# Encoder layer on one core: the last two gate chunks as block products, the retention heads started together, three task steps per unit

## The chip, the cores and the metric

The kernel runs on one core of a Trainium2 chip. The metric is device time in microseconds of one execution. The kernel before takes 1811.38 us (median of three runs, 1810.1 to 1811.63).

## What is computed

One encoder layer over 256 tokens of width 2048, all in float32:

```
h      = rmsnorm(x)
proj   = h @ w_in         -> q,k,v of the neighbourhood attention; q,k,v,gate of the retention;
                             q of the attention into mem; three branch gates of 2048 columns each
o_na   = neighbourhood_attention(...)             8 heads of 128
o_ret  = group_norm(retention both ways) * silu(gate)   8 heads, q/k of 128, v of 256
o_mem  = attention into rmsnorm(mem) @ w_mem_kv   4 heads of 256
merged = sigmoid(g_na) * (o_na @ w_br_na) + sigmoid(g_ret) * (o_ret @ w_br_ret)
         + sigmoid(g_mem) * (o_mem @ w_br_mem)
x      = x + merged @ w_out
x      = x + square(relu(rmsnorm(x) @ w_ff1)) @ w_ff2
```

The change touches the gates g_ret, the retention heads and the order of work around the three branch products.

## The kernel before

**Products and units.** Each float32 operand is split into a high and a low part (`split`, L92: ScalarE copies the high part, VectorE subtracts), and a product is three matmuls (`mm3`, L101: high by high, high by low, low by high). Weights come in 512 KB pieces of 256 rows by 512 columns. One piece for both halves of the tokens is a plain unit: 12 matmuls of 512 columns (`chunk`, L240; `do_mm`, L293). A chunk is 512 output columns; over 2048 rows it has 8 units.

**Block products.** `seven` (L656) computes two chunks at once by seven products of half-size blocks instead of eight, each over 4 pieces: 28 products of 6 matmuls each. For this VectorE adds and subtracts blocks of the activations once (`sums`, L781) and of the weights for every pair. Weight sums are formed partly by accumulating transfers into two rings of two buffers (`b1`, `b2`): a plain load from SP's queue, then one from POOL's queue that adds (`ring_load`, `ring_add`, L670 to L676). The last of them is issued with the split of product m6 (`pre`, L730) and is read by the split of product m7. The order is m1 x4, then per piece m3, m5, m7 of the piece before, m6, m2, m4, and m7 of the last piece at the end. While a set runs, six of the eight PSUM banks belong to it (`open_banks`).

**The list of units.** All units stand in one list, and the loop at the end of the function walks it: for unit i it issues the load of unit i + 4, the split of unit i + 2, runs hooks put at i (`at`, L881), the matmuls of unit i and then `run_tasks(i)`. The order is: attention chunks and the chunks on mem; 16 plain retention units; five sets of block products for the gates of the first two branches and half of the third (140 products), with the other 80 retention units spread among them; two plain gate chunks (16 units, `gate_plain`, L842) for the rest of the third branch's gates; the first branch product (na, 16 units), the second (mem, 16), the third (ret, 32); w_out; the feed-forward, where ff2's plain units are spread among the block products of ff1 in the same way. The gates and the retention's q, v and g go out to DRAM (`spill`) and come back when used (`fetch`); the first two branches' inputs too (`back`, L149), by a hook eight units ahead of the branch. Loads with the split operands' type go through POOL's queue, the others through SP's.

**Tasks.** Work that isn't matmuls of the list is written as generators. Each step names what it wants next ("ps" or "pt", the two kinds of PSUM bank, or nothing) and how many units it must wait; `run_tasks` (L216) gives at most two steps after each unit, and at most one for each kind of bank. A retention group (`ret_group`, L500) fetches its four buffers, waits four units, makes decay factors, takes two steps of transposes, then spawns its two heads and the next group. A head (`ret_head`, L517) has four steps: start, scores, output with group norm (in which VectorE waits for POOL's power step, L167 and L168), transposes. Head h is first read by unit h of the third branch. The first group starts three units behind the block products. The buffers of 4 KB a partition ("quad") are 30.

What the code issues in this order has that order of priority; the framework places an instruction earlier on its queue where its inputs and a buffer are free.

Of the kernel before, what the change touches and what calls it, by code (L numbers as in the profile page):

```python
# [12 lines left out]
F32 = mybir.dt.float32  # L13
F32R = mybir.dt.float32r
AF = mybir.ActivationFunctionType
# [6 lines left out]
NT = S // P  # L22
KT = D // P
# [34 lines left out]
def encoder_layer(ctx: ExitStack, tc: tile.TileContext, a, out):  # L58
    nc = tc.nc
# [32 lines left out]
    def split(hi, lo, src, scale=None):  # L92

        if scale is None:
            nc.scalar.activation(hi, src, AF.Copy)  # L95
            nc.vector.tensor_tensor(lo, src, f(hi), op=ALU.subtract)  # L96
        else:
            nc.scalar.activation(hi, src, AF.Copy, scale=scale)  # L98
            nc.vector.scalar_tensor_tensor(lo, src, scale, f(hi), op0=ALU.mult, op1=ALU.subtract)
# [13 lines left out]
    def quad(name, dt=F32R):  # L113

        return qp.tile([P, 4, S], dt, name=name, tag="quad")
# [4 lines left out]
    def spill(t, name):  # L120

        d = dram.tile([P, 4 * S], F32, name=f"d_{name}")
        nc.sync.dma_start(d, f(t).rearrange("p a s -> p (a s)"))
        return d

    def fetch(d, name, dt=F32):
        t = quad(name, dt)
        (nc.sync if dt == F32 else nc.gpsimd).dma_start(t.rearrange("p a s -> p (a s)"), d)
        return t

    def by_tok(t):

        return t.rearrange("p a s -> p (a s)").rearrange("p (t c) -> p t c", t=NT)

    class Lhs:
# [17 lines left out]
        def at(self, k, n=None, tok=slice(None)):  # L153

            ks = k % 4 if n is None else slice(k % 4, k % 4 + n)
            return [t[:, ks, tok] for t in self.quads(k // 4)]
# [19 lines left out]
    hT = Lhs("hT")  # L176
    r_x = const.tile([P, 8], F32, name="r_x")
# [33 lines left out]
    def spawn(gen, after=()):  # L211
        t = Task(gen, after)
        tasks.append(t)
        return t

    def run_tasks(now, n=2):  # L216

        given = set()
        for t in list(tasks):
            if n == 0:  # L220
                break
            if t.ready(now) and t.want not in given:
                if t.want is not None:
                    given.add(t.want)
                t.step(now)
                n -= 1
                if t.done:
                    tasks.remove(t)

    units = []  # L230
# [9 lines left out]
    def chunk(w, x, nkt, done, to=None, halves=False):  # L240

        nu = nkt // UK
        state = {"halves": halves}
        for u in range(nu):
            (units if to is None else to).append((w, u, x, u * UK, u == 0, u == nu - 1, done, state))
# [66 lines left out]
    def transposes(src, blocks):  # L312
        pt = ps_t.tile([P, 4, P], F32, name="pt")
        for j, b in enumerate(blocks):
            nc.tensor.transpose(pt[:, j, :], src[:, b * P:(b + 1) * P], ident)  # L315
        return pt

    def new_T(name):
        return [quad(f"{name}_{x}") for x in ("hi", "lo")]
# [147 lines left out]
    def decay_factors(g):  # L467

        lg, Fd, V = na_env["lg"], na_env["Fd"], nc.vector
        e1, e2 = cst["dist_f"], cst["dist_b"]  # L470
        Fq = quad("Fd", F32).rearrange("p a s -> p (a s)")
        for h in (2 * g, 2 * g + 1):
            t = t2f("junk")[:, :3 * P]
            Fd[h] = Fq[:, (h % 2) * 3 * P:(h % 2 + 1) * 3 * P]
            V.tensor_scalar_mul(t, e1, lg[:, h:h + 1])
            V.scalar_tensor_tensor(t, e2, lg[:, RET_H + h:RET_H + h + 1], t, op0=ALU.mult, op1=ALU.add)
            nc.scalar.activation(t, t, AF.Exp)
            V.tensor_scalar_mul(Fd[h], t, RET_QK ** -0.5)
# [16 lines left out]
            nc.vector.tensor_tensor(qv[:, :, 0, :], qv[:, :, 0, :], bv[:, :, 0, :], op=ALU.subtract)  # L495
            nc.vector.tensor_tensor(qv[:, :, 1, :], qv[:, :, 1, :], bv[:, :, 1, :], op=ALU.add)

    ret_dram = {}

    def ret_group(g):  # L500

        q2 = by_tok(fetch(ret_dram["q", g], "ret_q"))
        v = [by_tok(fetch(d, f"ret_v_{x}", F32R)) for d, x in zip(ret_dram["v", g], ("hi", "lo"))]
        gs = by_tok(fetch(ret_dram["g", g], "ret_gs"))
        yield None, 4
        decay_factors(g)
        T = new_T("ret_qkT")
        for t in range(NT):
            yield "pt", 1
            pt = transposes(q2[:, t, :], range(4))  # L510
            split(T[0][:, :, t * P:(t + 1) * P], T[1][:, :, t * P:(t + 1) * P], pt)
        for j in range(2):
            spawn(ret_head(2 * g + j, j, T, v, gs, env["oT_ret"]))
        if g + 1 < 4:
            spawn(ret_group(g + 1))

    def ret_head(h, j, qkT, v, gs, oT):  # L517
        Fd = na_env["Fd"]
# [39 lines left out]
    def w_chunk(name, c):  # L558
        return a[name][c]
# [27 lines left out]
    def win(c):  # L587
        return w_chunk("w_in", c)
# [233 lines left out]

    gate_dram = {}

    def put_gate(key, sg):
        yield None, 2
        gate_dram[key] = spill(sg, "sg")

    def gate_pair(key, c, ci, to):
        def finish(e):  # L830
            sgs = [quad("sg", F32) for _ in range(2)]
            for n, sign, ch, t in RESULTS:
                nc.scalar.activation(by_tok(sgs[ch])[:, t, :], e[n], AF.Sigmoid, scale=sign)
                if n == "c12":
                    yield None, 2
            for i in range(2):
                yield None, 2
                gate_dram[key, c + i] = spill(sgs[i], f"sg_{key}{c + i}")

        seven(win(ci), win(ci + 1), x_left, False, r_x, finish, to)  # L840

    def gate_plain(key, c, ci):  # L842
        def done_gate(acc):
            sg = quad("sg", F32)
            for t in range(NT):
                nc.scalar.activation(by_tok(sg)[:, t, :], acc[t], AF.Sigmoid, scale=r_x[:, t:t + 1])
            spawn(put_gate((key, c), sg))

        chunk(win(ci), hT, KT, done_gate)

    def ret_chunks(g, to):
        def put(key, ts, x=""):
# [36 lines left out]
    ret = ret[16:]  # L889
    sv = []  # L890
    for key, c, ci in (("w_br_na", 0, 8), ("w_br_na", 2, 10), ("w_br_mem", 0, 12), ("w_br_mem", 2, 14),
                       ("w_br_ret", 0, 28)):
        gate_pair(key, c, ci, sv)
    n = len(ret)
    for i, x in enumerate(sv):
# [6 lines left out]
        bank.clear()  # L902

    at(len(units) + 1, end_of_seven)
    at(len(units) + 3, lambda: spawn(ret_group(0)))
    for i in range(2):
        gate_plain("w_br_ret", 2 + i, 30 + i)


    def branch(wname, oT_key, nkt, first, last):  # L910
# [153 lines left out]
    for p in range(1, NPAIR):  # L1064
        sv = []
        ff1_pair(p, sv)
        for i, x in enumerate(sv):
            units.append(x)
            if p == 1:
                n = (i + 1) * (16 - LAG) // len(sv) - i * (16 - LAG) // len(sv)  # L1070
            elif i < EARLY:
                n = (i + 1) * LAG // EARLY - i * LAG // EARLY
            else:
                j, m = i - EARLY, len(sv) - EARLY
                r = 16 - LAG - (5 if p == NPAIR - 1 else 0)
                n = (j + 1) * r // m - j * r // m
# [12 lines left out]
    for i in range(n_units):  # L1089
        issue(i + LOADS)  # L1090
        do_split(i + SPLITS)
        for j in range(i, min(i + LEAD + 1, n_units)):
            if isinstance(units[j], Product):
                for lead, fn in units[j].acts:
                    if lead == j - i:
                        fn()
        if i == 20:
            spawn(stats_task(a["mem"], r_m))
        if i == 28:
            spawn(mem_task())  # L1100
        if i == 100:
            spawn(decay_task())
        if i == u_out - 4:
            for c in range(4):
                env["x1", c] = quad_f("x1")
                nc.gpsimd.dma_start(env["x1", c],
                                    a["x"][:, c * CW:(c + 1) * CW].rearrange("(t p) d -> p t d", p=P))
        for fn in hooks.get(i, []):
            fn()
        do_mm(i)  # L1110
        units_done.append(i)
        run_tasks(i)
    i = n_units
    while tasks:
        run_tasks(i)
        i += 1
# [102 lines left out]
```

## Time and profile before

| what | value |
|---|---|
| runs | 1810.1, 1811.38, 1811.63 us |
| the profiled execution | 1808.42 us |
| its span, first to last instruction | 1806.7 us |
| mean granted TensorE clock | 0.998 |
| TensorE, VectorE, ScalarE, POOL busy | 1778.9, 1411.2, 1043.7, 148.5 us |
| moved by DMA | 442.62 MB, 245 GB/s over the span |

TensorE is busy for nearly the whole span, so the table alone does not say where time could come from: for that one reads the idle stretches of TensorE, and how near the other engines are to their limit in each stage. Busy time is the union of an engine's instructions, which overlap at their ends: a matmul of 512 columns lasts some 0.39 us by its own row, and the next one starts sooner.

### The profile page before, as it was taken

The page shows a single profiled execution, that of the slowest core. Times are in us where ns is not written, and L with a number is a line of the kernel's source. Part 1 is how long each engine was busy: PE and PEld are TensorE (multiplying, and loading weights), DVE is VectorE, ACT ScalarE, POOL GpSimd, SP SyncE. Part 2 cuts the span into 40 slices and gives each one's busy share as a digit, 9 for nine tenths or more (in the row PEclk, how much of TensorE's full clock was granted, in tenths as well). Part 3 has the DMA queues.
Part 4 walks back from the last instruction along what each step waited for, and adds up shares of the span by engine and source line. Part 5 has one row for each costly group of instructions (what it writes and reads, how often), then busy time and mean ns, then how long its engine had stood idle before and what let it go on. Part 6 is the DMA issues. An engine that isn't in the chain of part 4 may idle for free.

```text
span 1806.7 us, 22753 instructions
## 1 busy us (share of the span) xinstructions
PE 1778.9 (98%) x8130; PEld 1467.8 (81%) x8130; DVE 1411.2 (78%) x1793; ACT 1043.7 (58%) x1305; POOL 148.5 (8%) x176
## 2 busy tenths in 40 slices
PE   8999999999999999999999999999999999999999
PEld 6888888787888887888788888777888888888877
DVE  6777766988788888868875556887898888888874
ACT  7665554556565665654434455855565656666552
POOL 0101000010001000101010000010111110110100
PEclk9999999999999999999999999999999999999999
DMA  9756555899998999987676555788889888888854
GB/s 328 270 202 229 187 175 198 271 292 293 279 301 239 312 289 279 297 315 284 230 254 211 185 184 180 223 243 222 244 256 267 232 266 246 252 237 281 221 186 140
DMA packets 148866, 442.62 MB, mean 245 GB/s; under 512 B 14096, under 2 KB 14608, under 8 KB 148752
## 3 DMA queue, kind: packets, MB, share of 16 engines
q1 hardware_dynamic: 123952, 377.54, 59.1%
q0 software_dynamic: 24512, 62.92, 18.1%
q8 instruction: 64, 1.05, 0.2%
q10 hardware_dynamic: 288, 0.70, 0.1%
q14 instruction: 50, 0.41, 0.1%
HBM read 420.13 MB, written 20.97 MB: 244 GB/s over the span
## 4 chain that ended last, share of the span: by engine, by line
PE 84%; DVE 8%; DMA 4%; ACT 2%; issue 2%; POOL 0%; SPq 0%; DVEq 0%; ACTq 0%; POOLq 0%
PE acc L103 22%; PE acc L104 22%; PE acc L102 22%; PE ps L104 3%; PE ps L103 3%; PE ps L102 3%; DVE w_lo L96 3%; DMA b<-in_w_ff 3%; PE pt L104 2%; PE pt L102 2%; PE pt L103 2%; ACT w_hi L95 1%; DMA raw<-in_w_ff 1%; PE pt L315 1%; DVE b L680 0%
## 5 line engine op out<-in xcount | busy, mean ns | idle before, releaser
L96 DVE TENSOR_TENSOR w_lo<-raw,w_hi 128x1024 fp32r<-128x1024 f32 (+1 forms) x545 | 660.4, 1221 | 202.5 <-ACT w_hi L95 196.7
L95 ACT ACTIVATE w_hi<-raw 128x1024 fp32r<-128x1024 f32 (+1 forms) x545 | 573.6, 1056 | 373.9 <-PE acc L104 287.6
L95 ACT ACTIVATE w_hi<-b 128x1024 fp32r<-128x1024 f32 x240 | 252.4, 1059 | 261.7 <-PE acc L104 142.7
L96 DVE TENSOR_TENSOR w_lo<-b,w_hi 128x1024 fp32r<-128x1024 f32 x240 | 291.8, 1223 | 114.5 <-ACT w_hi L95 111.9
L102 PE MATMUL acc<-w_hi,hT_hi 128*128 128x512 f32 x744 | 291.8, 394 | 7.6 <-ACT hT_hi L98 5.0
L103 PE MATMUL acc<-w_lo,hT_hi 128*128 128x512 f32 x744 | 291.2, 392 | 4.1 <-DVE w_lo L96 4.1
L104 PE MATMUL acc<-w_hi,hT_lo 128*128 128x512 f32 x744 | 290.5, 391 | 0.0
L103 PE MATMUL acc<-w_lo,fT_hi 128*128 128x512 f32 x512 | 200.7, 392 | 2.3 <-DVE w_lo L96 2.2
L102 PE MATMUL acc<-w_hi,fT_hi 128*128 128x512 f32 x512 | 201.1, 393 | 1.7 <-DVE x L1041 1.3
L104 PE MATMUL acc<-w_hi,fT_lo 128*128 128x512 f32 x512 | 200.1, 391 | 0.0
L102 PEld LDWEIGHTS acc<-w_hi,hT_hi 128*128 128x128 f32 x744 | 140.2, 189 | 37.3 <-ACT hT_hi L98 5.0
L103 PEld LDWEIGHTS acc<-w_lo,hT_hi 128*128 128x128 f32 x744 | 140.3, 189 | 34.0 <-DVE w_lo L96 6.0
L104 PEld LDWEIGHTS acc<-w_hi,hT_lo 128*128 128x128 f32 x744 | 140.2, 188 | 29.3
L103 PEld LDWEIGHTS acc<-w_lo,fT_hi 128*128 128x128 f32 x512 | 96.6, 189 | 24.7 <-DVE w_lo L96 4.9
L102 PEld LDWEIGHTS acc<-w_hi,fT_hi 128*128 128x128 f32 x512 | 96.5, 189 | 22.9 <-DVE x L1041 1.3
L104 PEld LDWEIGHTS acc<-w_hi,fT_lo 128*128 128x128 f32 x512 | 96.6, 189 | 20.0
L664 POOL DMA_DIRECT2D b<-in_w_ff x56 | 67.7, 1255 | 540.9 <-DMA b<-in_w_ff 162.3
L102 PE MATMUL pt<-w_hi,f_S_hi 128*128 128x512 f32 x192 | 75.0, 390 | 1.6 <-ACT w_hi L95 1.6
L103 PE MATMUL pt<-w_lo,f_S_hi 128*128 128x512 f32 x192 | 75.1, 391 | 0.8 <-DVE w_lo L96 0.8
L104 PE MATMUL pt<-w_hi,f_S_lo 128*128 128x512 f32 x192 | 75.0, 390 | 0.0
L664 POOL DMA_DIRECT2D b<-in_w_in x40 | 34.7, 896 | 429.9 <-DMA b<-in_w_in 321.0
L680 DVE TENSOR_TENSOR b<-b,raw 128x1024 f32<-128x1024 f32 x48 | 58.7, 1223 | 2.2 <-DMA raw<-in_w_in 1.2
(295 smaller groups left out, 2939.6 us busy)
## 6 DMA issues: line engine op xcount, KB each, us to landing
raw<-in_w_in SPq DMA_DIRECT2D x215, 512.0 KB, 5.4
raw<-in_w_ff SPq DMA_DIRECT2D x200, 512.0 KB, 5.9
b<-in_w_ff SPq DMA_DIRECT2D x56, 512.0 KB, 5.6
b<-in_w_ff POOLq DMA_DIRECT2D x56, 512.0 KB, 8.5
b<-in_w_in SPq DMA_DIRECT2D x40, 512.0 KB, 5.5
b<-in_w_in POOLq DMA_DIRECT2D x40, 512.0 KB, 7.6
raw<-in_w_mem_kv SPq DMA_DIRECT2D x32, 512.0 KB, 3.2
raw<-in_w_br_ret SPq DMA_DIRECT2D x32, 512.0 KB, 3.7
```

Source lines behind the costliest of these rows:

```text
L95: nc.scalar.activation(hi, src, AF.Copy)
L96: nc.vector.tensor_tensor(lo, src, f(hi), op=ALU.subtract)
L102: nc.tensor.matmul(o, lhsT=lh, rhs=rh, start=start, stop=False)
L103: nc.tensor.matmul(o, lhsT=lh, rhs=rl, start=False, stop=False)
L104: nc.tensor.matmul(o, lhsT=ll, rhs=rh, start=False, stop=stop)
L315: nc.tensor.transpose(pt[:, j, :], src[:, b * P:(b + 1) * P], ident)
L664: eng.dma_start(t.rearrange("p (b c) -> p b c", b=2) if len(src.shape) == 3 else t, src, **kw)
L680: V.tensor_tensor(raw, raw, add, op=ALU.add)
```

## The change

The third branch's last two gate chunks are computed by a sixth set of block products, so that there are 168 products with the 80 retention units among them and no plain gate chunk. The unit behind the last product is then the first branch's first. `ret_group(0)` starts one unit behind the block products instead of three; each group spawns the next in its first step instead of its last, and waits three units instead of four before its decay factors. `ret_built` is an empty list to which nothing is added, so `ret_built[-1:]` names no task to wait for. `run_tasks` gives three steps per unit instead of two, in the whole kernel. The limit of one step for each kind of bank stays.

```
-    def run_tasks(now, n=2):
+    def run_tasks(now, n=3):
...
-    ret_dram = {}
+    ret_dram, ret_built = {}, []
...
         gs = by_tok(fetch(ret_dram["g", g], "ret_gs"))
-        yield None, 4
+        if g + 1 < 4:
+            spawn(ret_group(g + 1), ret_built[-1:])
+        yield None, 3
         decay_factors(g)
...
             spawn(ret_head(2 * g + j, j, T, v, gs, env["oT_ret"]))
-        if g + 1 < 4:
-            spawn(ret_group(g + 1))
...
     for key, c, ci in (("w_br_na", 0, 8), ("w_br_na", 2, 10), ("w_br_mem", 0, 12), ("w_br_mem", 2, 14),
-                       ("w_br_ret", 0, 28)):
+                       ("w_br_ret", 0, 28), ("w_br_ret", 2, 30)):
         gate_pair(key, c, ci, sv)
...
-    at(len(units) + 3, lambda: spawn(ret_group(0)))
-    for i in range(2):
-        gate_plain("w_br_ret", 2 + i, 30 + i)
+    at(len(units) + 1, lambda: spawn(ret_group(0)))
```

The functions `put_gate` and `gate_plain`, now unused, are removed.

## Rows read from the trace of the kernel before

**Rows 1.** The page, busy time, share of the span and instructions of TensorE.
```profile
PE 1778.9 (98%) x8130; PEld 1467.8 (81%) x8130; DVE 1411.2 (78%) x1793; ACT 1043.7 (58%) x1305; POOL 148.5 (8%) x176
```

**Rows 2.** Waits of TensorE, whole span: releaser, us in total, times, longest.
```profile
PE acc L103 <- DVE w_lo L96: 7.0, 7, 1.7
...
PE pt L552 <- DVE ret_qkT_lo L96: 3.6, 3, 1.4
...
PE acc L102 <- DVE junk L493: 1.4, 2, 0.7
```

**Rows 3.** Busy time by stretch; last columns granted clock, DMA share, GB/s.
```profile
335.00:766.40 431.40, 425.84 (x1873) 350.66 (x1872) 368.90 (x370) 261.12 (x273) 38.03 (x47) 1.00 0.92 287
766.40:926.00 159.60, 156.03 (x782) 130.75 (x780) 123.05 (x226) 75.98 (x95) 13.68 (x26) 1.00 0.74 270
1150.00:1240.00 90.00, 86.11 (x373) 68.92 (x372) 73.26 (x79) 54.76 (x67) 10.86 (x9) 0.97 0.90 254
1516.00:1608.00 92.00, 92.00 (x416) 76.20 (x415) 81.50 (x81) 57.41 (x62) 12.07 (x10) 1.00 0.87 250
```

**Rows 4.** TensorE in order of time: start, duration, line, operation.
```profile
762.29 0.39 PE L102 MATMUL pt<-w_hi,f_S_hi 128*128 128x512 f32 x1
...
766.14 0.39 PE L104 MATMUL acc<-w_hi,hT_lo 128*128 128x512 f32 x1
766.37 0.39 PE L102 MATMUL acc<-w_hi,hT_hi 128*128 128x512 f32 x1
...
815.36 0.40 PE L102 MATMUL acc<-w_hi,oT_na_hi 128*128 128x512 f32 x1
...
925.97 0.48 PE L102 MATMUL acc<-w_hi,oT_ret_hi 128*128 128x512 f32 x1
```

**Rows 5.** VectorE: splits in order of time; its wait for POOL; merges, 764 to 960.
```profile
903.54 4.63 DVE L96 TENSOR_TENSOR w_lo<-raw,w_hi 128x1024 fp32r<-128x1024 f32 x4
...
DVE rs_t L169 <- POOL rs_y L168: 8.6, 8, 1.1
...
L929 DVE TENSOR_TENSOR merged<-merged,junk 128x512 f32<-128x512 f32 x10 | 6.7, 686 | 0.0
```

**Rows 6.** DMA queues, 335 to 766 us: packets, MB, share of 16 engines.
```profile
q1 hardware_dynamic: 27180, 98.96, 62.1%
q0 software_dynamic: 6785, 24.72, 29.8%
```

**Rows 7.** POOL's accumulations (L664): landing 335 to 770, 1150 to 1240; one issue.
```profile
DMA to landing us min/median/max: 5.3/7.6/10.5
...
DMA to landing us min/median/max: 6.4/9.0/12.3
...
746.25 0.86 POOL L664 DMA_DIRECT2D b<-in_w_in  x1 [12.78 <-DVE b L680]
```

**Rows 8.** A set's end in the feed-forward: ScalarE, TensorE, then two stretches.
```profile
1230.71 1.06 ACT L95 ACTIVATE w_hi<-b 128x1024 fp32r<-128x1024 f32 x1 [6.14 <-DMA b<-in_w_ff]
...
1231.82 0.49 PE L102 MATMUL pt<-w_hi,f_S_hi 128*128 128x512 f32 x1 [1.59 <-ACT w_hi L95]
1233.07 0.50 PE L103 MATMUL pt<-w_lo,f_S_hi 128*128 128x512 f32 x1 [0.76 <-DVE w_lo L96]
...
1234.00:1236.00 2.00, 1.49 (x4) 0.61 (x2) 2.00 (x5) 1.75 (x3) 1.20 (x1) 0.50 0.81 261
...
1238.00:1240.00 2.00, 2.00 (x6) 1.52 (x6) 2.00 (x4) 1.28 (x2) 0.00 (x0) 0.50 1.06 250
```

**Rows 9.** The first branch's input: one issue on POOL; landing, median us.
```profile
748.37 0.90 POOL L128 DMA_DIRECT2D oT_na_lo<-d_oT_na_lo  x1
...
oT_na_lo<-d_oT_na_lo POOLq DMA_DIRECT2D x2, 512.0 KB, 15.1
```

**Rows 10.** POOL's first power step, 764 to 960 us: count, ns min/median/max.
```profile
L167 POOL TENSOR_SCALAR rs_u<-mv x8: 191/191/1069, 813.3 to 923.8; 128x2 f32<-128x2 f32 x8
```

More of the change, by code (lines that the diff above doesn't have):

```diff
@@ L823, in encoder_layer @@
     gate_dram = {}
-    def put_gate(key, sg):
-        yield None, 2
-        gate_dram[key] = spill(sg, "sg")
     def gate_pair(key, c, ci, to):
@@ L840, in gate_pair @@
         seven(win(ci), win(ci + 1), x_left, False, r_x, finish, to)
[L842 to L849, printed above, removed]
     def ret_chunks(g, to):
```

## The prediction

> **What bounds the kernel now.** I read the page's busy shares first, then who waits for whom on TensorE, then busy time by stage, and only then single instructions. TensorE is busy for 98% of the span [rows 1], and all that it waits for is some 25 us: in the stages that the change touches there are three waits of the last retention step for VectorE (3.6 us), two for an accumulator that VectorE has not emptied (1.4 us) and some late low halves of weights [rows 2]. The granted clock is 1.00 in these stages [rows 3]. So a matmul saved is time saved, as long as VectorE and the DMA keep up, and their margins decide the rest: in the stage of block products (335 to 766 us, with a few plain units ahead of them) VectorE is busy for 368.9 of 431.4 us and the DMA for 0.92; in the stage with the retention heads (766 to 926 us) VectorE has 123.05 us of work beside 156.03 us of TensorE's [rows 3]. I call the first unit after the block products L; in the kernel before it begins at 766.37 us, the first branch product at 815.36 us and the third at 925.97 us [rows 4].
>
> **1. Two plain gate chunks become one set of seven block products.** Eighteen matmuls of 512 columns start between 762.29 and 766.14 us, so one costs 3.85 / 17 = 0.2265 us, in a block product and in a plain unit alike [rows 4]. Plain: 2 chunks x 8 units x 12 matmuls = 192, or 43.5 us. Block products: 28 x 6 = 168, or 38.1 us. All lie on TensorE's path: **-5.4 us**.
>
> What comes with them: VectorE gets 28 splits and 8 adds of the same shape at 1.16 us and seven combinations at 0.67 us [rows 5], 46 us beside 38.1 us of matmuls, so its share of the stage goes from 0.855 to (368.9 + 46) / 469.5 = 0.88. The DMA took 2.71 us a MB for plain loads and 5.20 for the queue of accumulating ones (62.1% of 431.4 us for 98.96 MB, 29.8% for 24.72 MB [rows 6]); 16 loads and 8 accumulations of 0.524 MB are 22.7 + 21.8 = 44.5 us in 38.1, and the share goes from 0.92 to 0.94. Both stay covered on average.
>
> The Trainium skill (Perfetto Trace Analysis, section Roofline) names some 435 GB/s as the most that a core's 16 DMA engines move; by that the 287 GB/s of this stage would leave a third free and the late transfers of rival 3 would have no cause. The rows differ: the same engines are at 0.92 already, since an accumulated byte holds them nearly twice as long, so I keep the rival at its full chance.
>
> **2. The same 80 retention units among 168 products instead of 140.** Before, a plain unit follows the one before it after one or two products; now always after two or more (80 / 168 is under a half). The two waits for an emptied accumulator, 0.7 us each [rows 2], have 1.36 us more cover and go: -1.4 us. What is late next is the tail of each set. The last accumulation into the ring is issued with the sixth product's split, and the last product reads it. Before, three products and two plain units lie between, in every set: issue at 746.25, use at 762.29 us, 16 us [rows 4, 7]. Counted out for 168 products, four of the six sets lose one plain unit there: 13.3 us. The landing takes 5.3 to 10.5 us in this stage [rows 7], then ACT's and VectorE's split, some 2 us: still in time, by less than a microsecond at the worst. Bounds: 0, and four times the wait of the set in the feed-forward whose mixture is the same (13 plain to 28): 1.59 + 0.76 us [rows 8], 9.4 us. I take +1.0, near the 10.5 us of the same loads. Together **-0.4 us**.
>
> **3. The heads beside 32 units instead of 48.** The gate units that covered group 0 are gone. TensorE's work from L to the third branch is 156.03 - 43.5 = 112.5 us; VectorE's is 123.05 - 16 x 1.16 = 104.5 us, and 113.1 with the eight waits for POOL's power step, 8.6 us [rows 3, 5]. Before, these were 131.7 beside 156: VectorE's slack is what the change spends. Three steps a unit, with one scores step and one transpose step at most: group 0 is fetched at L+1, the others at L+2 to L+4 (nothing holds them back, the list for it stays empty); the first head's scores come at L+9, then a scores or output step in each unit to L+24, the last transpose at L+27. So the heads fit before they are read (head h at L+32+h), but between L+4 and L+24 VectorE has 104.5 less 11 splits (12.8) and three chunks of merges (ten operations at 0.67 us [rows 5], 6.7), 85.0 us, beside 112.5 - 11 x 2.72 = 82.6 us of TensorE: over by 2.4 us, by 11.0 if no work fills the POOL waits, less the 5.4 us of the two units whose weights lie split ahead. The thirty 4 KB buffers soften it: four groups at seven, two branches' inputs at four each, the merged sums and gates pass thirty from about L+8, so groups 2 and 3 slide by some three units into emptier ones. Idle: 0 at best, 11.0 at worst, against 3.6 now [rows 2]; I take 5.1, near today's and a little under the middle: **+1.5 us**.
>
> **4. The seam at L.** The first branch's four inputs come back eight units before its start: that was in the gate chunks, and is now among the block products. The slower half landed 15.1 us after issue there [rows 9]; eight units there (two products and a plain unit in turn, 5.4 us for three) are 14.5 us. Before, they were issued at some 748 us [rows 9], ahead of their place in the code, and I expect that again, since buffers come free then. Bounds: 0, and 7.5 us if they are issued in their place behind the ring's loads and wait another 7.6 us for them, the median landing of those [rows 7]; I take the side on which they were, **+0.3 us**. All POOL and SP issues that move (16 fetches of 0.5 MB in four units) stand behind this; at 0.74 DMA share [rows 3] they find room, and weights are loaded four units ahead.
>
> **5. Three steps a unit elsewhere.** Attention heads and the feed-forward's tasks take one scores and one transpose step a unit as before, and fewer than three are usually ready; TensorE waits for none of them now [rows 2]. I take **0**, between -1 and +2 (the waits of late low halves there).
>
> **Sum.** -5.4 - 0.4 + 1.5 + 0.3 = -4.0 us, against the profiled execution's 1808.42 (span 1806.7 and 1.7 around it): 1804.4. The median of the timed runs is 3.0 us above that execution, so **1807.4 us**.
>
> **Rivals.** *1, more than the gain:* beside the two accumulator waits the three head waits of 3.6 us also go, since four groups in flight leave TensorE other work; -5.4 - 1.4 - 3.6 = -10.4, 1801.0. For it: these waits are VectorE's, caused by one group at a time. Against: VectorE's margin shrinks in both stages.
>
> *2, VectorE bounds the heads (slower):* the place is L+4 to L+24, the mechanism the sum of part 3 without its cushions. It decides once VectorE's work there exceeds TensorE's by more than the 5.4 us split ahead. Price: 11.0 us of idle instead of 5.1, plus POOL's step held back: of eight rs_u of 191 ns one took 1069 [rows 10]; 0.88 x 8 heads = 7.0. Change: -4.0 + 5.9 + 7.0 = +8.9, 1820.3; without POOL's part 1813.3, with half of it 1816.8. Against it: three units of slide are as good as certain, and VectorE can fill a POOL wait with a split. The Trainium skill (SBUF — State Buffer, section Who interferes with whom) says that a VectorE instruction with two SBUF inputs and a GpSimd one that reads SBUF exclude each other for the whole instruction. The one long rs_u is what that would look like; by that rule the 7.0 us would come in full wherever VectorE never pauses.
>
> *3, the ring's tail:* one of the four shortened sets lands as late as 12.3 us [rows 7]. In the feed-forward this idled TensorE for 2.35 us, and then the granted clock stood at 0.50, the lower level, from about 1234 to 1240 us [rows 8], 3 us more: 5.4 us for one set: 1812.8; for two 1818.2. For it: the same mixture there, in a stage with a lower DMA share [rows 3]. Against: 10.5 us is the worst of 39 here, and the set with 16 plain units to 28 at 1516 us waits for nothing [rows 3].
>
> *4, it does not do what it says:* the buffers run out, the later groups wait and are fetched one after the other as now; the heads end at the third branch, and -5.4 is returned as waits there: 1811.
>
> **How the numbers follow.** Forecast (1805 to 1810): 0.45. Rival 1 (1801 to 1805): 0.14. Rival 2 (1813 to 1820): 0.20. Rival 3 (1810 to 1818): 0.14. Rival 4 (1810 to 1813): 0.07. A measurement tells 0.2% apart, 3.6 us: faster is below 1807.8, slower above 1815.0. Faster: all of rival 1 and six tenths of the forecast, 0.42. Slower: two thirds of rival 2 and some of rival 3, 0.21. Same: 0.37. The range 1801 to 1818 leaves out the upper third of rival 2 and a little at the other end; the forecast's own range is 1805 to 1810.
>
> **What would show it.** Right: TensorE's groups for the gate weights lose 24 matmuls; the block-product stage is 38 us longer with no accumulator wait behind the rotated queries; L to the third branch takes 114 to 119 us, with VectorE above 90%. Wrong: idle before the last product of a set with ACT waiting for the ring's DMA, and a clock of 0.5 behind it (rival 3); waits for low halves of weights between the first and second branch (rival 2); a wait at the first matmul of the first branch (part 4); new waits before 335 us (part 5).

## The result, and the profile after

The changed kernel takes 1831.87 us (median of four runs, 1829.71 to 1838.85), the kernel before beside it 1810.98: ratio 1.0111, 95% interval 1.0092 to 1.0131. The forecast was 1807.4 us, its range ended at 1818. The profiled execution takes 1830.54 us, its span is 22.1 us longer than before. By stage, read in the two traces from the start of one matmul to the start of another; "work moved" is what the change shifts between the stages at 0.2265 us a matmul, "lost" is the rest:

| stage | before | after | more | work moved | lost |
|---|---|---|---|---|---|
| start to the first block product | 353.2 | 357.3 | +4.1 | 0 | +4.1 |
| block products, to the last one | 409.8 | 469.2 | +59.4 | +38.1 | +21.3 |
| from there to the first matmul of w_out | 253.5 | 213.0 | -40.5 | -43.5 | +3.0 |
| the rest | 790.1 | 789.2 | -0.9 | 0 | -0.9 |

Behind the last block product there still stands one plain retention unit, as before; the first branch's first unit begins at 829.89 us and the third branch's at 948.59.

The page's first rows, against [rows 1]: 24 matmuls fewer, as forecast, yet TensorE is busy 4.8 us longer: matmuls behind a wait start further apart, as shown below, some of them at the lower clock.

```profile
PE 1783.7 (98%) x8106; PEld 1464.7 (80%) x8106; DVE 1431.9 (78%) x1820; ACT 1052.2 (58%) x1316; POOL 160.3 (9%) x184
```

TensorE's waits in the stage of block products after the change (releaser, us, times, longest). Before, there were four waits with 3.9 us in all, of the kinds in the first line here (2.5 us) and the last (1.4 us).

```profile
PE acc L103 <- DVE w_lo L96: 6.7, 6, 1.3
PE pt L102 <- ACT w_hi L95: 3.5, 4, 1.8
PE pt L103 <- DVE w_lo L96: 3.4, 5, 0.8
PE ps L103 <- DVE w_lo L96: 0.9, 2, 0.5
PE ps L102 <- ACT w_hi L95: 0.6, 1, 0.6
PE acc L102 <- DVE junk L493: 0.3, 1, 0.3
```

The largest new ones are `pt`, most of them product m7 at the end of a set. The first set's end shows the chain. POOL, ScalarE and TensorE (start, duration, operation; in brackets the idle time before it and its releaser), three views:

```profile
414.72 1.75 POOL L664 DMA_DIRECT2D b<-in_w_in  x2 [16.02 <-DMA b<-in_w_in]
```
```profile
427.49 1.06 ACT L95 ACTIVATE w_hi<-b 128x1024 fp32r<-128x1024 f32 x1 [6.36 <-DMA b<-in_w_in]
```
```profile
428.60 0.54 PE L102 MATMUL pt<-w_hi,f_S_hi 128*128 128x512 f32 x1 [1.82 <-ACT w_hi L95]
429.86 0.80 PE L103 MATMUL pt<-w_lo,f_S_hi 128*128 128x512 f32 x1 [0.72 <-DVE w_lo L96]
```

POOL issued two accumulations one behind the other. In its queue the first is the next set's first one (ring `b1`); it waited for its plain load until 414.72 us, and behind it stood this set's last (ring `b2`), whose input VectorE had finished at 413.15 us:

```profile
411.92 1.23 DVE L680 TENSOR_TENSOR b<-b,b 128x1024 f32<-128x1024 f32 x1
```

The time from issue to landing, of the first of the two alone, then of both (min, median, max):

```profile
DMA to landing us min/median/max: 8.8/8.8/8.8
...
DMA to landing us min/median/max: 8.8/10.5/12.1
```

So the second was issued at 415.3 and landed at 427.4 us, and ScalarE, idle for 6.36 us, took it at once. Over the whole stage the accumulations' median rose from 7.6 [rows 7] to 8.7 us, the longest from 10.5 to 12.1:

```profile
DMA to landing us min/median/max: 5.4/8.7/12.1
```

Then the clock: ten microseconds around this end had a granted clock of 0.66 of full speed on average, that is partly the lower level of 1.2 GHz, behind the idle shown (columns as in [rows 3]).

```profile
426.00:436.00 10.00, 7.40 (x19) 4.86 (x18) 7.42 (x9) 5.99 (x7) 0.86 (x1) 0.66 0.78 215
```

I add up by how much the distance from one matmul's start to the next exceeds 0.2265 us: in the whole stage 25.9 us against 4.9 before, which is nearly the loss of 21.3. Three of the four shortened set ends hold 12.7 of the 25.9 (6.1 at 426 to 436 us, 3.3 at 584 to 592, 3.3 at 665 to 672), with the plain unit behind each, whose low half VectorE splits late because it had waited too. At the second and third of them the granted clock stayed at 1.00. Another 4.5 us, at 592 to 603, lie close behind the third set's end but have another cause: the set's last combinations and a retention chunk's rotation (L489 to L496) fill VectorE, and the next split comes late. The clock was 0.50 from 600 to 603 us.

```profile
593.33 0.69 DVE L756 TENSOR_TENSOR c<-pt,u 128x512 f32<-128x512 f32 x1
...
598.47 0.43 DVE L496 TENSOR_TENSOR ret_q<-ret_q,junk 128x256 f32<-128x256 f32 x1
598.80 2.36 DVE L96 TENSOR_TENSOR w_lo<-raw,w_hi 128x1024 fp32r<-128x1024 f32 x2
```
```profile
600.09 0.79 PE L103 MATMUL acc<-w_lo,hT_hi 128*128 128x512 f32 x1 [1.24 <-DVE w_lo L96]
```

The two sets that kept their plain unit lose nothing at their end, nor does the last set, behind which no set comes. That last set loses 2.9 us earlier, at 811 to 815 us, in products of its third and fourth piece: POOL had fetched the first branch's four inputs from 779 us on and then stood behind a plain load of the ring.

```profile
779.27 0.89 POOL L128 DMA_DIRECT2D oT_na_hi<-d_oT_na_hi  x1
...
800.51 1.78 POOL L664 DMA_DIRECT2D b<-in_w_in  x2 [18.75 <-DMA b<-in_w_in]
```

The loss at the start is one longer wait and the lower clock behind it (0.53 of full speed from 340.4 to 343.8 us). TensorE, before:

```profile
337.05 0.50 PE L103 MATMUL acc<-w_lo,hT_hi 128*128 128x512 f32 x1 [1.67 <-DVE w_lo L96]
```

and after:

```profile
339.64 0.50 PE L103 MATMUL acc<-w_lo,hT_hi 128*128 128x512 f32 x1 [3.98 <-DVE w_lo L96]
```

VectorE before had the weight's split ahead of the next sums of the activations (a task's step), and after the change behind them, two views:

```profile
335.76 1.24 DVE L96 TENSOR_TENSOR w_lo<-raw,w_hi 128x1024 fp32r<-128x1024 f32 x1
...
338.62 0.77 DVE L789 TENSOR_TENSOR s<-xt_in 128x256 f32<-128x256 f32 x2
```
```profile
336.69 0.42 DVE L96 TENSOR_TENSOR f_S_lo<-s,f_S_hi 128x256 fp32r<-128x256 f32 x1 [0.49 <-ACT f_S_hi L95]
337.03 0.42 DVE L789 TENSOR_TENSOR s<-xt_in,s 128x256 f32<-128x256 f32 x1
337.36 1.09 DVE L96 TENSOR_TENSOR f_S_lo<-s,f_S_hi 128x256 fp32r<-128x256 f32 x3
338.37 1.22 DVE L96 TENSOR_TENSOR w_lo<-raw,w_hi 128x1024 fp32r<-128x1024 f32 x1
```

### The profile page after: what moved, and what is told of

Its sections match the earlier page's. It is cut to its first block, busy times and chain, and to the rows that moved or that the text cites. A ratio compares the mean times of both kernels' runs of the same rounds, so it can differ in the third digit from the quotient of the medians.

```text
span 1828.8 us, 22815 instructions
## 1 busy us (share of the span) xinstructions
PE 1783.7 (98%) x8106; PEld 1464.7 (80%) x8106; DVE 1431.9 (78%) x1820; ACT 1052.2 (58%) x1316; POOL 160.3 (9%) x184
## 4 chain that ended last, share of the span: by engine, by line
PE 75%; DVE 9%; DMA 9%; ACT 3%; issue 3%; POOL 1%; SPq 0%; DVEq 0%; ACTq 0%; POOLq 0%
PE acc L103 19%; PE acc L104 19%; PE acc L102 19%; DVE w_lo L96 5%; DMA b<-in_w_in 4%; PE ps L103 3%; PE ps L104 3%; PE ps L102 3%; ACT w_hi L95 2%; PE pt L103 2%; PE pt L104 2%; PE pt L102 2%; DMA b<-in_w_ff 1%; DMA raw<-in_w_br_na 1%; DMA raw<-in_w_ff 1%
## 5 line engine op out<-in xcount | busy, mean ns | idle before, releaser
L96 DVE TENSOR_TENSOR w_lo<-raw,w_hi 128x1024 fp32r<-128x1024 f32 (+1 forms) x537 | 649.5, 1220 | 181.0 <-ACT w_hi L95 176.1
L95 ACT ACTIVATE w_hi<-b 128x1024 fp32r<-128x1024 f32 x260 | 272.8, 1058 | 286.7 <-PE acc L104 154.8
L96 DVE TENSOR_TENSOR w_lo<-b,w_hi 128x1024 fp32r<-128x1024 f32 x260 | 315.3, 1223 | 138.8 <-ACT w_hi L95 136.4
L103 PE MATMUL acc<-w_lo,hT_hi 128*128 128x512 f32 x688 | 272.3, 396 | 10.4 <-DVE w_lo L96 10.3
L102 PE MATMUL acc<-w_hi,hT_hi 128*128 128x512 f32 x688 | 272.1, 397 | 6.3 <-ACT hT_hi L98 4.9
L104 PE MATMUL acc<-w_hi,hT_lo 128*128 128x512 f32 x688 | 270.8, 394 | 0.0
L103 PEld LDWEIGHTS acc<-w_lo,hT_hi 128*128 128x128 f32 x688 | 130.9, 190 | 40.8 <-DVE w_lo L96 14.9
L102 PEld LDWEIGHTS acc<-w_hi,hT_hi 128*128 128x128 f32 x688 | 131.0, 190 | 34.4 <-ACT hT_hi L98 4.9
L104 PEld LDWEIGHTS acc<-w_hi,hT_lo 128*128 128x128 f32 x688 | 130.9, 190 | 27.5
L664 POOL DMA_DIRECT2D b<-in_w_ff x56 | 67.8, 1297 | 539.8 <-DVE b L680 144.9
L664 POOL DMA_DIRECT2D b<-in_w_in x48 | 41.8, 935 | 486.7 <-DMA b<-in_w_in 358.7
L680 DVE TENSOR_TENSOR b<-b,b 128x1024 f32<-128x1024 f32 x52 | 63.6, 1224 | 1.3
```

What stands on the lines that cost most here:

```text
L102: nc.tensor.matmul(o, lhsT=lh, rhs=rh, start=start, stop=False)
L103: nc.tensor.matmul(o, lhsT=lh, rhs=rl, start=False, stop=False)
L104: nc.tensor.matmul(o, lhsT=ll, rhs=rh, start=False, stop=stop)
L664: eng.dma_start(t.rearrange("p (b c) -> p b c", b=2) if len(src.shape) == 3 else t, src, **kw)
L680: V.tensor_tensor(raw, raw, add, op=ALU.add)
```

## The experiments

Three theories of the loss: the ring's tail (the last accumulation of a set), three steps a unit at the start, and the heads; the rival to all is that a sixth set simply asks too much of VectorE or the DMA. Each ratio is to runs of the kernel before on the same chip, with its 95% interval. 0.1% is 1.8 us. As an estimate from the intervals, the difference of two ratios is uncertain by some 0.15% where both kernels have eleven runs or more, and by some 0.25% where the changed kernel with its four takes part.

**One part alone: three steps** (`run_tasks(now, n=3)` in the kernel before).

> The kernel before with three task steps per unit and nothing else. Theory (a: the time lost is at the ends of the sets, where the last accumulation lands late, and in the one wait at 335 us that came with three steps a unit): 2 to 5 us slower than before, about 1814.5, with a wait for a low half of a weight of some 4 us at about 335 us where before had 1.7. Rival (b: three steps a unit cost nothing, all of the loss lies in the sixth set): 1811, no change.

Measured 1.0034 (1.0023 to 1.0046), 1817.1 against 1811.4 us. The wait is there to the hundredth, and the stage up to the first product is 4.1 us longer, as in the changed kernel. In this trace the block products take 3.5 us longer too; whether that is the third step or scatter was not separated.

```profile
339.71 0.80 PE L103 MATMUL acc<-w_lo,hT_hi 128*128 128x512 f32 x1 [3.98 <-DVE w_lo L96]
```

**That part taken back up to the end of the block products.**

```
+    seven_end = [10 ** 6]
...
-    def run_tasks(now, n=3):
+    def run_tasks(now):
+        n = 3 if now >= seven_end[0] else 2
...
+    seven_end[0] = len(units)
```

> The changed kernel with two task steps per unit up to the end of the block products and three from there on. Theory (a): the wait at about 335 us returns to 1.7 us, with the clock behind it: 3 to 5 us less than the changed kernel, about 1828; the set ends stay. Rival (b, the number of steps does not matter there): 1832.

1.0077 (1.0061 to 1.0094), 0.34% less than the changed kernel: the price seen the other way round, not far above the uncertainty. The wait is back at 1.68 us; the block products still take 469.3 us.

```profile
337.36 0.50 PE L103 MATMUL acc<-w_lo,hT_hi 128*128 128x512 f32 x1 [1.68 <-DVE w_lo L96]
```

**Two plain units in every tail.** The same 80 units, by written patterns instead of evenly:

```
+    mix13 = "0101010101010100101010101010"
+    mix14 = "0101010101010101101010101010"
+    for x, m in zip(sv, (mix13 + mix13 + mix14) * 2):
...
+        if m == "1":
             units.append(ret.pop(0))
```

A 1 puts a plain unit behind the product.

> The changed kernel with the same 80 plain units among the same 168 products, but placed so that in each of the six sets two plain units lie between product m6 and product m7 of the last piece (now one, in four of six). Theory (a, the ring's tail): the 20 us lost at the ends of the four shortened sets go for the most part, 14 to 20 us less than the changed kernel, 1812 to 1818. Rival (b, VectorE and the DMA are overloaded in the whole stage by the sixth set): no change, 1830 to 1834, the idle moves to other places. Rival (c, half of it: the accumulation is late because another stands ahead of it on POOL's queue, and one more plain unit is only just enough): 7 to 14 us less.

1.0065 (1.0051 to 1.0079): 0.46% or 8.3 us less than the changed kernel, the half that rival (c) expected. Every wait of m7 is gone, though the set's last accumulation still stands behind the next set's first (at 495 us it took 12.3 us to land). What remains is mostly waits of plain units, two of them on weights that had not landed:

```profile
PE acc L103 <- DVE w_lo L96: 6.1, 6, 1.5
PE acc L102 <- ACT w_hi L95: 2.7, 2, 1.6
PE ps L103 <- DVE w_lo L96: 0.6, 1, 0.6
```

**The tail off the ring.** The last piece's `b2` is completed by a plain load and an addition on VectorE, in the sets of the gates (there `r` is not None):

```
-                ring_add("b2", k, w2[k])
+                if k < NK - 1 or r is None:
+                    ring_add("b2", k, w2[k])
...
+            if k == NK - 1 and r is not None:
+                return Product(mm, [(L_LOAD, lambda: raw_load(("r7", k), w2[k])),
+                                    (L_SPLIT, lambda: do(("s7", k), ring["b2"][k % 2], e.pop(("r7", k))))])
```

> The changed kernel, in whose six sets the last piece of the second ring is no longer completed by an accumulating transfer on POOL's queue but by a plain load from SP's queue and one addition on VectorE (6 additions of 1.23 us more on VectorE, 6 accumulations fewer). Theory (a, the ring's tail): the idle at the four set ends goes, with the half clock behind it: 16 to 21 us less than the changed kernel, 1811 to 1816. Rival (b, VectorE is the bound of the stage): 7.4 us more work for VectorE, so 1832 to 1840.

1.0039 (1.0026 to 1.0052): 0.72% or 13.0 us less. The stage shrinks by 14.9 to 454.4 us although VectorE has 4.5 us more to do there (394.46 against 389.98), so VectorE's total was not the bound. At the first set's end nothing is lost now (425 to 440 us); beside the rotation at the third set's end 3.8 us still are. The first window is the changed kernel's, the second this one's.

```profile
357.26:826.50 469.24, 453.61 (x1955) 367.85 (x1954) 389.98 (x376) 278.65 (x288) 47.35 (x59) 0.99 0.92 280
```
```profile
358.53:812.92 454.39, 448.34 (x1954) 366.55 (x1953) 394.46 (x381) 278.37 (x287) 41.98 (x53) 1.00 0.93 293
```

**Only the queue ahead of the tail.** The first piece's `b1` on VectorE instead, the tail still a transfer (the same lines, for m5 and k = 0).

> The changed kernel, in whose sets the first piece of the first ring is completed by a plain load and one addition on VectorE instead of an accumulating transfer, so that on POOL's queue nothing of the next set stands ahead of a set's last accumulation any more; that last accumulation itself stays a transfer, and one plain unit still covers it. Theory (a1, the last accumulation is late because it is issued behind the next set's first one and shares the DMA with it): it is issued 1 to 2 us sooner and lands 6 to 9 us after issue instead of 11.3 to 12.1, so the waits at the first set ends go: 9 to 14 us less than the changed kernel, 1818 to 1823, near the 1819 of the kernel with VectorE's addition. Rival (a2, one plain unit is too little whatever stands on the queue): landings stay at 11 us, no more than 4 us less, 1828 to 1832.

1.0082 (1.0066 to 1.0098): 0.29% or 5 us less, below the expectation and hardly above the uncertainty. Its mechanism shows in the trace: with nothing of the next set ahead, the first set's last accumulation is issued as soon as VectorE is done, lands in 7.3 us, and TensorE waits for nothing there.

```profile
417.40 0.86 POOL L664 DMA_DIRECT2D b<-in_w_in  x1 [15.46 <-DVE b L680]
```
```profile
DMA to landing us min/median/max: 7.3/7.3/7.3
```

At the next four ends it took 7.1 to 8.3 us. The loss in the last set stays, 3.0 us. And VectorE's additions now fall at the start of a set, beside the combinations of the set before, and there are new waits (2.0 us more than the normal step at 362 us, others at 521, 605 and 752 to 762). So queue order explains the late landing, and this way of mending it gives back only a part.

**Both repairs together.**

> The changed kernel with VectorE's addition at the end of each set and two task steps per unit up to the end of the block products. If the two losses are separate they add: 1831.9 - 12.8 - 5.8 = 1813.3 (1811 to 1816), and what is left above the forecast of 1807.4 lies in VectorE's bursts at the set ends and in the heads. If both edits cured the same thing: 1817 to 1820.

1.0028 (1.0019 to 1.0037), 0.83% less than the changed kernel, where the two alone make 1.06%; that difference is within the uncertainty. The start is as before (354.5 us), the stage of block products at 456.7 no shorter than with the first repair alone; 13.5 us are lost in it. The largest place, with 3.8 us, is the end of the third set, where the changed kernel lost 4.5 us. VectorE there, from a combination of the set (L759) through all of a retention chunk's rotation (L491 to L498) to the next split:

```profile
580.03 0.69 DVE L759 TENSOR_TENSOR c<-pt,u 128x512 f32<-128x512 f32 x1
580.64 0.74 DVE L491 SCALAR_TENSOR_TENSOR ret_q<-acc,r_x,c_tables 128x512 f32<-128x512 f32 x1
581.29 0.74 DVE L696 SCALAR_TENSOR_TENSOR u<-acc,r_x,u 128x512 f32<-128x512 f32 x1
...
585.18 0.42 DVE L498 TENSOR_TENSOR ret_q<-ret_q,junk 128x256 f32<-128x256 f32 x1
585.52 2.36 DVE L96 TENSOR_TENSOR w_lo<-raw,w_hi 128x1024 fp32r<-128x1024 f32 x2
```

**The chunks in another order**, so that these two do not meet.

```
-        for i, done in enumerate((done_qk, done_v, done_g)):
...
+        for i in ((0, 1, 2), (1, 2, 0), (1, 0, 2), (1, 0, 2))[g]:
```

> The kernel before this one in the list, with the chunks of three retention groups in another order, so that no chunk of queries and keys ends (ten VectorE instructions of rotation, 4.9 us) where a set of block products ends (seven combinations of 0.68 us). Theory (what is left of the loss in the block products is VectorE's bursts where the two meet, waits for an accumulator and for low halves of 1.1 to 1.7 us): 3 to 6 us less than without the new order, 1808 to 1811. Rival (VectorE is short of time in the whole stage, the waits only move): the same as without, 1813.

0.9988 (0.9974 to 1.0001): 0.4% or 7 us less than without the new order. The stage takes 451.0 us, at full clock, with 8.0 us lost.

```profile
352.92:803.87 450.95, 445.55 (x1954) 365.80 (x1953) 396.48 (x384) 279.37 (x288) 42.15 (x53) 1.00 0.94 298
```

VectorE's total is nearly the same (396.5 against 395.3 us); only where it falls changed.

**The heads one after the other**, in the kernel with both repairs, and in the changed kernel alone:

```
-        if g + 1 < 4:
-            spawn(ret_group(g + 1), ret_built[-1:])
         yield None, 3
...
             spawn(ret_head(2 * g + j, j, T, v, gs, env["oT_ret"]))
+        if g + 1 < 4:
+            spawn(ret_group(g + 1))
```

> The same kernel as the second of this list, but with the retention groups one after the other again, each spawned when the one before has its transposes (first start, wait of three units and three steps as changed). Theory (the 32 units need the groups side by side): the last heads are late for the third branch, TensorE waits some 8 to 16 us there: 1821 to 1829. Rival (the heads fit serially too, since three steps a unit are enough): 1813.

0.9993 (0.9983 to 1.0004): my theory was wrong; it is 0.35% or 6 us less than side by side. Its profiled execution, 1819.9 us, was the slowest of twelve, so the changed kernel gives a second pair:

> The changed kernel with only the retention groups put back one after the other (start one unit behind the block products, three steps a unit). Theory (the side-by-side start loads VectorE and costs 3 to 6 us, and the heads fit without it): 1826 to 1829. Rival (here, with the ring's last transfers still late, the groups need the side-by-side start): 1832 or more, with waits at the third branch.

1.0088 (1.0073 to 1.0103), 0.23% or 4 us less, which these runs alone do not tell from nothing. From the last block product to w_out, first the changed kernel, then this one, it is 4.9 us less; VectorE is busy for 1.3 us less there.

```profile
826.50:1039.54 213.04, 208.19 (x1016) 172.30 (x1015) 161.21 (x276) 95.04 (x118) 16.01 (x24) 1.00 0.70 253
```
```profile
827.92:1036.02 208.10, 206.04 (x1017) 172.82 (x1016) 159.95 (x275) 96.29 (x118) 17.98 (x25) 1.00 0.72 258
```

Up to the third branch TensorE waited, side by side, for score banks and late weights as well:

```profile
PE ps L102 <- DVE z L545: 1.8, 3, 0.9
PE acc L103 <- DVE w_lo L96: 1.5, 2, 0.8
PE pt L552 <- DVE rs_y L172: 1.0, 1, 1.0
PE pt L315 <- DVE ret_qkT_lo L96: 0.3, 1, 0.3
PE acc L102 <- ACT w_hi L95: 0.2, 1, 0.2
```

and one after the other for the heads' transposes alone:

```profile
PE pt L552 <- DVE z L547: 2.1, 3, 1.1
```

**All repairs, and the same tail in the feed-forward.**

> The kernel with VectorE's addition at each set's end, two steps a unit up to the end of the block products and the new order of the retention chunks, and with the retention groups one after the other again. If the side-by-side start of the groups costs what the two traces show in the stage of the heads (213.0 against 210.4 us) or what the medians show (1817.8 against 1811.3), this takes 2.6 to 6.5 us less than 1810.6: 1804 to 1808, faster than the kernel before. Rival (the difference between those two medians was scatter): 1810.

0.9980 (0.9967 to 0.9994): faster than the kernel before, 1808.09 against 1812.94 us. Against the same kernel with the groups side by side, it is 0.08% less, which these runs do not tell apart. In the traces the stage from the last block product to w_out is shorter one after the other in all three pairs: by 4.9 us here above, 2.6 with both repairs, 3.8 with all.

> The same with VectorE's addition also at the end of each set of block products in the feed-forward. Theory (the first of those sets waits for its last accumulation too, some 2 us and the half clock behind it): 3 to 6 us less than the kernel before it in this list, 1800 to 1804. Rival (that wait stands before the accumulator of ff2, which is late for another reason, and the clock falls anyway): no change.

0.9949 (0.9934 to 0.9963), 1802.01 us: 0.31% less again. The wait at the first such set in the feed-forward, the one of [rows 8], is 2.24 us without this addition,

```profile
1229.03 0.50 PE L102 MATMUL pt<-w_hi,f_S_hi 128*128 128x512 f32 x1 [2.24 <-ACT w_hi L95]
1230.29 0.50 PE L103 MATMUL pt<-w_lo,f_S_hi 128*128 128x512 f32 x1 [0.76 <-DVE w_lo L96]
```

and gone with it; the stage from the first ff1 product to the end goes from 650.1 to 643.9 us. This version beats both kernels.

## Why the prediction was wrong

*Part 1, -5.4 us:* right. 24 matmuls are gone, and once the waits were repaired 168 products and 80 units take 445.6 us of TensorE (the window under the new order of the chunks), at the forecast 0.2265 us a matmul.

*Part 2 is the step that failed.* I wrote of the shortened tails "The landing takes 5.3 to 10.5 us in this stage, then ACT's and VectorE's split, some 2 us: still in time, by less than a microsecond at the worst", and took +1.0 us. It measured 12.7 us, at three of the four, and without the transfer at the tail it was gone. The place was right, the size was not. The 16 us between issue and use were read at the last set, 746.25 us, the one set behind which no other comes; its landing took 6.8 us, and that end held in the changed kernel too. At the other four set ends of the kernel before, the next set's first accumulation stood ahead, and three of the four tails took 10.2 to 10.3 us. The first of them, two issues one behind the other:

```profile
414.56 1.75 POOL L664 DMA_DIRECT2D b<-in_w_in  x2 [12.02 <-DMA b<-in_w_in]
```

So the worst landing was no outlier but the rule for a tail; on top came up to 2 us in the queue, and landings of 11.3 to 12.1 us at the three ends. The Trainium skill (SBUF — State Buffer, section "Can I just issue two DMAs to hit both halves?") says that two concurrent transfers serialize on the same engines. The trace agrees: the pair was issued 0.6 us apart and landed 3.9 us apart, and the accumulation without the other took 7.3 us. My bound, four times 2.35 us, counted only the wait itself. Rival 3 priced a late set with the clock at 5.4 us; the three cost 6.1, 3.3 and 3.3, and the clock fell only at the first. Its mechanism came true; its number of sets, one or two, was too small and the chance, 0.14, too low. The saved accumulator waits came (1.4 to 0.3 us), but the waits for low halves behind the rotations did not go. Counted by the distances between matmuls, some 10 us are now lost outside the tails and the last set, 4.5 of them at the third set's end, against 4.9 in the whole stage before. The sum of part 2 has no term for that, and the new order of the chunks took back part of it.

*Part 3, +1.5:* +3.0 in the trace, inside its bounds. That the heads fit was right: from L, the first branch's first unit, to the third branch it took 118.7 us (forecast 114 to 119), with 4.1 us of idle (forecast 5.1), and VectorE was busy for 103.6 us of it, 87% and not above 90. What I did not weigh was the start side by side itself: one after the other, the stage to w_out is 2.6 to 4.9 us shorter. Which of VectorE's order and the crowded DMA makes it dearer was not separated. Rival 2's share for POOL came only in part: three of the eight rs_u were long (1140 to 1142 ns), against one in [rows 10], yet VectorE's wait for POOL fell from 8.6 to 6.4 us. The Trainium skill (SBUF — State Buffer, section Who interferes with whom) says that a VectorE instruction with two SBUF inputs contends with a GpSimd instruction that reads SBUF. The long rs_u are what that would look like, but they did not set the time: one after the other four of the eight were long, and the stage was shorter. Rival 4 expected the heads to be late one after the other; with three steps a unit they were not, and with two it was not tried.

*Part 4, +0.3:* the branch's inputs came in time, issued early as expected. The last set loses 2.9 us beside them; that they are the cause is argued from their place and not shown, since with two plain units in every tail, and with the new order of the chunks, they come back in the same set and its third and fourth piece lose nothing. With the tails' 12.7 us and the 5 us more behind VectorE this makes the 21 us of the stage.

*Part 5, 0:* wrong by 4 us in one stage of the traces, by 6 us in the medians of three steps alone; the other 2 us were not placed. I took what TensorE waits for now as harmless, also beside the sums of the activations at 326 to 343 us, where VectorE was already late (1.67 us) and a third step puts more of its work ahead of a split.

## What to carry to other kernels

Take a margin from every instance of a pattern, not from one, and look what stands ahead in the queue: the last member of a series can have a neighbour fewer, as here. When work is saved from TensorE, the units that go are also distance for transfers, and an addition on an engine with room can be cheaper than a transfer that needs that distance. A small task that falls where another burst of the same engine ends costs time although the engine has room on average. A limit of steps per unit guards the order of work on VectorE; raise it only where the time is needed.

## What was not expected of the hardware

The same stage varies from execution to execution: VectorE, ScalarE and SP have the same order of instructions in the block products of the two kernels with and without side-by-side heads (both repairs), yet their profiled executions took 456.7 and 463.2 us. Twelve runs of one kernel spread over 11 us (1808.92 to 1819.91), so that a change of 0.2% needs many runs and a trace. What makes the executions differ stays open.
